# When a residual stream kept by columns is read back by rows: the read-back and the first output columns' evacuation moved in a hand-kept order

## The chip, the cores and the metric

The kernel runs on one core of one Trainium2 chip. The metric is the device time of one execution, in microseconds; the runs of the kernel before took 957.2 (median of 3; 956.22 to 961.8). Traces are of one profiled execution; their times count from the start of its span.

## The reference

Two layers of a decoder trunk on x of 256 tokens x 1024 features, all in f32:

```python
for l in range(DEPTH):                     # DEPTH = 2
    x = x + 0.5 * swiglu(rmsnorm(x, ffn1_norm[l]), ffn1_w_gate[l], ffn1_w_up[l], ffn1_w_down[l])
    ...                                    # a token mixer, then attention on a memory of 256 rows
    x = x + 0.5 * swiglu(rmsnorm(x, ffn2_norm[l]), ffn2_w_gate[l], ffn2_w_up[l], ffn2_w_down[l])
return rmsnorm(x, final_norm)

def swiglu(x, w_gate, w_up, w_down):
    return (jax.nn.silu(x @ w_gate) * (x @ w_up)) @ w_down
```

The hidden width of each SwiGLU is 2816, that is 22 tiles of 128. The change lies in the very last of these stages, ffn2 of layer 1, with the final rmsnorm behind it.

## The kernel before, in words

**Precision and weights.** Each f32 product is made of three fast ones: both sides are split into a high part and a rest. The weights stream through one ring: SP's queue loads chunks of 1 MB into tiles named raw (4 buffers, `_load_to`, L113 to L118, three chunks ahead), and for each block of 8 weight tiles ACT writes the high part whi (L143) and DVE the rest wlo (L144), five blocks deep. A block can be split when PE has let go of the block five before it. PE then runs three matmuls for each product (L575 to L577 in the gate and up products, L684 to L686 in some of them, L791 to L793 in the down product of the last stage).

**The residual x** is kept with features on the partitions and tokens along them. The last stage is different: its down product (`down_tok`, L769) puts tokens on the partitions, so that the rows of the result can be written out directly. For that x itself is needed by tokens. This is done in three steps: `to_tokens` (L508) turns two feature tiles at a time on DVE in 32x32 pieces and stores them on SP's queue into a DRAM tile, tok (L514, four times); `from_tokens` (L836) reads tok back with four DMAs on POOL's queue (L839) into a tile of the name bias; `natural(k)` (L844) copies each of the eight feature tiles k, for both halves of the tokens u, on ACT (L847) into the tile y, which has the name k2 and appears as k in the trace.

**The hidden tiles h** take a similar way. When a group of four (the last: two) hidden tiles is there by tokens, `turned_back` (L540) turns it on DVE (L545), stores it to a DRAM tile, turn (L547), reads it back with four DMAs (L549, all on POOL's queue), and some time later splits it on ACT and DVE into h (L557, L558). The six groups use the tile names v, kT, v, k2, kT, v in turn.

**The down product** has two column halves. First columns 0 to 511, for u = 0 and 1, two hidden tiles at a time: eleven parts; part i needs h of hidden tiles 2i and 2i + 1, so the eleventh part needs the group that is turned last. Then columns 512 to 1023: one long part for the first 14 hidden tiles (three regions: u = 0 whole, u = 1 in two halves of 256), and the last eight hidden tiles region by region. `evac_tok` (L800) evacuates a finished region: it adds half of the product to y (L804), sums y's squares (L807), multiplies by the final gain (L810 on POOL for the first columns), and, with the last region of a row, raises the mean to the power -1/2 on POOL (L813), scales (L817 on ACT, L820 on DVE) and writes out (L818, L821).

**What sets the order.** `Order` (L200) writes the program out with a clock of its own. Fillers are the parts of the products, each with a cost in ns (L582, L690, L798); a task given to `pe.after(delay, fn, cost)` runs, between two fillers, once the clock has passed its due time; of several due tasks the one with the earlier due time comes first. A part of the down product is not started before its h tiles have been split (`have`, L741). In the last stage the clock starts at 0 with the first gate product. Each of the 43 fillers of the gate and up products costs 2600; the norm's sums cost 250; a part of the first down columns costs 2616; the long part of the other columns 14 x 1308.

The order in which the instructions are written is not fully the order in which they run: when the program is built, a scheduler orders each engine's instructions by its own estimates of when their inputs are there, and takes the one written first when several are. An instruction wrapped in `tc.keep_in_program_order` is held behind the instruction that was written just before it on its engine. The read-back DMAs (L839) and the splits of h (L557, L558) are held so; the copies (L847), the evacuation and, in this stage, the weight splits are not.

Due times around the change, in ns of the order's clock: `from_tokens` 93000 after the stage's start; `natural(k)` 27000 + 1500 k after `from_tokens` ran; the split of the last two groups of h 22000 after they were turned; the evacuation of a region at once, with the part that finishes it.

Of the kernel before, what the change touches and what calls it, by code (L numbers as in the profile page):

```python
# [240 lines left out]
def paired(t):  # L241

    return t.rearrange("p (b a) -> p a b", b=2)
# [22 lines left out]
def build(nc, tc, ctx, a):  # L266
# [18 lines left out]
    def w2():  # L285
        return act.tile([P, 512], F32, name="w2", bufs=6)
# [28 lines left out]
    pe = Order()  # L315
# [192 lines left out]
    def to_tokens(tok, k):  # L508


        t = act.tile([P, 2 * S], F32, name="q2", bufs=2)
        tc.keep_in_program_order(nc.vector.transpose(t.rearrange("q (a g j) -> q g a j", a=4, g=4),
                                                     x[:, k:k + 2].rearrange("p k (u a i) -> p (k u) a i", u=2, a=4)))
        tc.keep_in_program_order(nc.sync.dma_start(tok[k // 2], t))  # L514
# [19 lines left out]
    def ffn(which, layer, n, nxt, first=False, last=False):  # L534
# [206 lines left out]
        def have(ks):  # L741
            return lambda: math.inf if any(h[k] is None for k in ks) else 0.0
# [26 lines left out]
        def down_tok():  # L769

            late = 2 * (ws.BUFS - 1)
            pss, got, mean = {}, {}, [EPS, EPS]

            def part(fs, *regions):

                c = regions[0][1] // 512

                def go():  # L780
                    for f in fs:
                        if (f, c) not in got:
                            got[f, c] = ws.take(f"{which}_w_down", layer, f * P, c * 512, 4)
                        for reg in regions:
                            u, c0, c1 = reg
                            if f == 0:
                                pss[reg] = (sc_tile if c == 1 and c1 - c0 == 512 else acc_tile)()[:, :c1 - c0]
                            ps = pss[reg]
                            wh, wl = (paired(w)[:, (c0 - c * 512) // 2:(c1 - c * 512) // 2] for w in got[f, c])
                            hh, hl = (h[f].v[:, u, m] for m in range(2))  # L790
                            nc.tensor.matmul(ps, hh, wh, start=f == 0, stop=False)  # L791
                            nc.tensor.matmul(ps, hh, wl, start=False, stop=False)
                            nc.tensor.matmul(ps, hl, wh, start=False, stop=f == FT - 1)  # L793
                    if fs[-1] == FT - 1:
                        for u, c0, c1 in regions:
                            evac_tok(u, slice(c0, c1), pss[u, c0, c1])

                return have(fs), go, sum(len(fs) * (c1 - c0) * 654 // 512 for _, c0, c1 in regions)  # L798

            def evac_tok(u, at, ps):  # L800
                xtok = back["y"]
                y = xtok[:, u, at]
                g = gfin[at.start // 512][:, at.start % 512:at.start % 512 + at.stop - at.start]
                nc.vector.scalar_tensor_tensor(y, ps, 0.5, y, op0=ALU.mult, op1=ALU.add)  # L804
                ms = act.tile([P, 1], F32, name="mean", bufs=4)
                junk = w2()[:, :at.stop - at.start]
                nc.vector.tensor_tensor_reduce(junk, y, y, 1.0 / D, mean[u], ALU.mult, ALU.add, ms)  # L807
                mean[u] = ms
                if at.stop < D:
                    nc.gpsimd.tensor_tensor(y, y, g, op=ALU.mult)  # L810
                    return
                r = act.tile([P, 1], F32, name="rcol", bufs=2)
                nc.gpsimd.tensor_tensor(r, ms, mhalf[:, 0:1], op=ALU.pow)  # L813
                nc.vector.tensor_tensor(y, y, g, op=ALU.mult)
                out = a["out"][u * P:(u + 1) * P]
                cuts = (0, 384, 704, D)
                nc.scalar.activation(xtok[:, u, :cuts[1]], xtok[:, u, :cuts[1]], AF.Copy, scale=r)  # L817
                nc.scalar.dma_start(out[:, :cuts[1]], xtok[:, u, :cuts[1]])  # L818
                for i, j in zip(cuts[1:], cuts[2:]):
                    nc.vector.tensor_scalar(xtok[:, u, i:j], xtok[:, u, i:j], r, None, op0=ALU.mult)  # L820
                    nc.sync.dma_start(out[:, i:j], xtok[:, u, i:j])  # L821

            end = range(FT - late, FT)
            right = ((0, 512, D), (1, 512, 768), (1, 768, D))
            return [part(range(i, i + 2), (0, 0, 512), (1, 0, 512)) for i in range(0, FT, 2)] + [
                part(range(FT - late), *right)] + [part(end, reg) for reg in right]
# [5 lines left out]
        if last:  # L832
            gfin = []
            tok, back = dram.tile([KT // 2, P, 2 * S], F32, name="tok"), {}

            def from_tokens():  # L836
                t = act.tile([P, 2 * D], F32, name="bias", bufs=1)
                for b in range(4):
                    tc.keep_in_program_order(nc.gpsimd.dma_start(  # L839
                        t[32 * b:32 * b + 32].rearrange("i (g z) -> i g z", g=16),  # L840
                        tok.rearrange("k (p i) (a z) -> a i (k p) z", p=4, a=4)[b]))
                v = t.rearrange("q (k p m u j) -> q u k m p j", k=4, p=4, m=2, u=2)

                def natural(k):  # L844
                    y = back["y"] = back.get("y") or act.tile([P, 2, D], F32, name="k2", bufs=1)
                    for u in range(2):
                        nc.scalar.activation(y[:, u, k * P:(k + 1) * P].rearrange("q (p j) -> q p j", p=4),  # L847
                                             v[:, u, k // 2, k % 2], AF.Copy)

                for k in range(KT):  # L850
                    pe.after(27000 + 1500 * k, lambda k=k: natural(k), 0)

            def last_factors():
                gfin.extend(act.tile([P, 512], F32, name="p2", bufs=4) for _ in range(2))
                src = a["final_norm"]
                for i, g in enumerate(gfin):
                    nc.sync.dma_start(g, bass.AP(tensor=src.tensor, offset=src.offset + i * 512, ap=[[0, P], [1, 512]]))

            pe.after(90000, last_factors, 0)
            for k in range(0, KT, 2):  # L860
                pe.after(16000 + 9000 * (k // 2), lambda k=k: to_tokens(tok, k), 0)
            pe.after(93000, from_tokens, 0)
        at = AT.get((which, layer))
        groups = [f0 for f0 in range(0, FT, 4) if at is None or f0 != SEVEN]
        ups = [f for f0 in groups for f in hidden(f0)]
# [504 lines left out]
    pe.after(60000, mem_scale, 0)  # L1370
    pe.after(100000, lambda: early.update(bias=load_bias(0)), 0)
    ffn("ffn1", 0, n, nxt, first=True)
    bias, sinks = early["bias"], (vecs[:, VCOL["sinks"]:VCOL["sinks"] + 8], nsinks)

# [11 lines left out]
    memory(0, n, nxt, keys[0])  # L1386
    n, nxt = nxt, xn(("ffn1_norm", 1))
    ffn("ffn2", 0, n, nxt)
    n, nxt = nxt, xn(("mix_norm", 1))
    pe.after(114000, lambda: early.update(bias=load_bias(1)), 0)  # L1390
    ffn("ffn1", 1, n, nxt)
    n, nxt = nxt, xn(("xa_norm", 1))
    odd_mixer(n, nxt, early["bias"], mem_keys(1))
# [73 lines left out]
```

## Time and profile before

| what | value |
| --- | --- |
| median of the runs | 957.2 us (956.22, 957.2, 961.8) |
| the profiled execution's own time | 956.5 us |
| its span | 954.5 us |
| granted TensorE clock, mean over the span | 0.998 |
| PE busy | 945.7 us, 99% |
| DVE busy | 726.4 us, 76% |
| ACT busy | 596.8 us, 63% |
| POOL busy | 118.0 us, 12% |
| DMA, mean | 247 GB/s |

How to read the rows that follow. In an order of time a row has the start in us, the duration in us, the engine, the line, the operation, output<-input with the program's tile names, the shapes, xN for N instructions run together, and in brackets the idle time of the engine just before it and what ended that. In a table by stretch each row has the stretch, its length, then for PE, PEld (the weight loads), DVE, ACT and POOL the busy us and the number of instructions, then the granted TensorE clock, the DMA share and GB/s. In the chain of waits a row has start, duration and what the end of the program was waiting for at that time. "DMA to landing" is the time from the issue of a DMA to the landing of its last byte.

### The profile page before, as it was taken

The numbers are of one execution on the slowest core, as the hardware profiler recorded it, in microseconds if no ns is written. First come the engines' busy times: TensorE is split into PE (matmuls) and PEld (weight loads), VectorE is DVE, ScalarE is ACT, GpSimd is POOL, SyncE is SP. The second block draws the span as 40 slices with busy tenths as digits, with TensorE's granted clock in tenths as the row PEclk, the third lists the DMA queues.
The fourth block names the chain that finished last, engine by engine and source line by source line (L and its number), as shares of the span: only waits on it lengthen the run. The fifth ranks groups of instructions, "written<-read, shape, count | busy, mean of one in ns | idle before, by whom it ended". The sixth has DMA issues, their size and how long they took to land.

```text
span 954.5 us, 15174 instructions
## 1 busy us (share of the span) xinstructions
PE 945.7 (99%) x5796; PEld 866.9 (91%) x5796; DVE 726.4 (76%) x1153; ACT 596.8 (63%) x984; POOL 118.0 (12%) x207
## 2 busy tenths in 40 slices
PE   9999999999999999999999999999999999999997
PEld 8888899999999888889988888999999998888896
DVE  7667667798878886976778697687877789769583
ACT  7555555697657865655577565456785688565551
POOL 0412210001000110221001111200000001202311
PEclk9999999999999999999999999999999999999999
DMA  9999875455536889989768978855644388999851
GB/s 369 330 357 322 311 234 218 170 187 195 184 134 243 231 259 301 302 290 349 245 196 242 333 246 270 323 200 181 239 147 167 113 288 259 292 322 329 255 189 45
DMA packets 39368, 235.44 MB, mean 247 GB/s; under 512 B 5624, under 2 KB 6648, under 8 KB 14720
## 3 DMA queue, kind: packets, MB, share of 16 engines
q1 hardware_dynamic: 26928, 182.43, 52.1%
q0 software_dynamic: 11792, 51.42, 20.5%
q8 instruction: 45, 0.74, 0.3%
q10 hardware_dynamic: 576, 0.64, 0.2%
q14 instruction: 27, 0.22, 0.1%
HBM read 220.81 MB, written 16.80 MB: 249 GB/s over the span
## 4 chain that ended last, share of the span: by engine, by line
PE 95%; DMA 2%; ACT 1%; DVE 0%; POOL 0%; issue 0%; POOLq 0%; SPq 0%; DVEq 0%; ACTq 0%
PE acc L576 11%; PE acc L577 11%; PE acc L575 11%; PE acc L418 8%; PE acc L423 7%; PE acc L425 7%; PE acc L424 7%; PE acc L419 4%; PE sc L418 3%; PE tr L685 2%; PE tr L684 2%; PE tr L686 2%; PE sc L575 2%; PE sc L576 2%; PE sc L577 2%; PE sc L419 2%
## 5 line engine op out<-in xcount | busy, mean ns | idle before, releaser
L144 DVE TENSOR_TENSOR wlo<-raw,whi 128x1024 fp32r<-128x1024 f32 (+2 forms) x363 | 409.4, 1140 | 153.9 <-ACT whi L143 151.4
L143 ACT ACTIVATE whi<-raw 128x1024 fp32r<-128x1024 f32 (+2 forms) x363 | 353.4, 986 | 238.4 <-PE acc L577 81.8
L576 PE MATMUL acc<-wlo,x 128*128 128x512 f32 x528 | 200.5, 380 | 0.2
L577 PE MATMUL acc<-whi,x 128*128 128x512 f32 x528 | 199.9, 379 | 0.0
L575 PE MATMUL acc<-whi,x 128*128 128x512 f32 x528 | 195.3, 380 | 0.0
L576 PEld LDWEIGHTS acc<-wlo,x 128*128 128x128 f32 x528 | 99.8, 189 | 15.7 <-DVE wlo L144 1.7
L575 PEld LDWEIGHTS acc<-whi,x 128*128 128x128 f32 x528 | 99.7, 189 | 14.1 <-ACT whi L143 0.2
L577 PEld LDWEIGHTS acc<-whi,x 128*128 128x128 f32 x528 | 99.8, 189 | 14.0
L418 PE MATMUL acc<-h,whi 128*128 128x512 f32 x330 | 108.6, 382 | 0.0
L419 PE MATMUL acc<-h,wlo 128*128 128x256 f32 x330 | 89.9, 273 | 0.0
L425 PE MATMUL acc<-h,wlo 128*128 128x256 f32 x322 | 87.7, 275 | 0.0
L424 PE MATMUL acc<-h,whi 128*128 128x256 f32 x322 | 87.7, 275 | 0.0
L423 PE MATMUL acc<-h,whi 128*128 128x256 f32 x322 | 86.5, 277 | 0.0
L425 PE MATMUL acc<-x,wlo 128*128 128x256 f32 x304 | 84.1, 278 | 0.0
L424 PE MATMUL acc<-x,whi 128*128 128x256 f32 x304 | 83.8, 277 | 0.0
L423 PE MATMUL acc<-x,whi 128*128 128x256 f32 x304 | 83.3, 278 | 0.0
L418 PEld LDWEIGHTS acc<-h,whi 128*128 128x128 f32 x330 | 62.4, 189 | 8.6
L419 PEld LDWEIGHTS acc<-h,wlo 128*128 128x128 f32 x330 | 63.3, 192 | 0.2
L424 PEld LDWEIGHTS acc<-h,whi 128*128 128x128 f32 x322 | 61.7, 192 | 0.1
L425 PEld LDWEIGHTS acc<-h,wlo 128*128 128x128 f32 x322 | 61.7, 192 | 0.1
L423 PEld LDWEIGHTS acc<-h,whi 128*128 128x128 f32 x322 | 60.6, 192 | 0.4 <-DVE x L486 0.2
L424 PEld LDWEIGHTS acc<-x,whi 128*128 128x128 f32 x304 | 58.2, 192 | 0.2
(274 smaller groups left out, 1730.8 us busy)
## 6 DMA issues: line engine op xcount, KB each, us to landing
raw<-in_w SPq DMA_DIRECT2D x165, 1024.0 KB, 6.8
bias<-in_w POOLq DMA_DIRECT2D x12, 1024.0 KB, 12.6
k<-in_w POOLq DMA_DIRECT2D x9, 1024.0 KB, 9.1
turn<-v POOLq DMA_DIRECT2D x9, 512.0 KB, 3.3
v<-turn POOLq DMA_DIRECT2D x36, 128.0 KB, 6.5
dists<-line POOLq DMA_DIRECT2D x2, 1536.0 KB, 14.1
raw<-in_memT SPq DMA_DIRECT2D x3, 1024.0 KB, 4.7
turn<-kT POOLq DMA_DIRECT2D x6, 512.0 KB, 10.6
```

Source lines behind the costliest of these rows:

```text
L143: for ins in (self.nc.scalar.activation(hi[:, at], src, AF.Copy), self.nc.vector.tensor_tensor(lo[:, at], src, hi[:, at].bitcast(F32), op= ...
L144: self.nc.vector.tensor_tensor(lo[:, at], src, hi[:, at].bitcast(F32), op=ALU.subtract)):
L418: nc.tensor.matmul(ps, w[0], x2.both, start=start, stop=False)
L419: nc.tensor.matmul(ps[:, :S], w[1], x2.high, start=False, stop=stop)
L423: nc.tensor.matmul(ps[:, :S], w[0], x2.high, start=start, stop=False)
L424: nc.tensor.matmul(ps[:, :S], w[0], x2.low, start=False, stop=False)
L425: nc.tensor.matmul(ps[:, :S], w[1], x2.high, start=False, stop=stop)
L575: nc.tensor.matmul(ps[u], xh, wh, start=k == 0, stop=False)
L576: nc.tensor.matmul(ps[u], xh, wl, start=False, stop=False)
L577: nc.tensor.matmul(ps[u], xl, wh, start=False, stop=k == KT - 1)
L684: nc.tensor.matmul(ps, xh, wh, start=p == 0, stop=False)
L685: nc.tensor.matmul(ps, xh, wl, start=False, stop=False)
```

## The change

Three delays in `ffn` change, all of them in the last stage. The read-back of x by tokens is due at 114500 in place of 93000, which is after the clock at which the last group of hidden tiles is turned. The copies are due 15000 + 700 k after the read-back in place of 27000 + 1500 k. The evacuation of a region is now a task of its own: due 6000 after the end of its part for the first columns (c = 0), and at once, but still as a task, for the others. No instruction is added or taken away.

```diff
@@ down_tok, part
                     if fs[-1] == FT - 1:
                         for u, c0, c1 in regions:
-                            evac_tok(u, slice(c0, c1), pss[u, c0, c1])
+                            pe.after(0 if c else 6000, lambda u=u, at=slice(c0, c1), ps=pss[u, c0, c1]: evac_tok(u, at, ps), 0)
@@ from_tokens
                 for k in range(KT):
-                    pe.after(27000 + 1500 * k, lambda k=k: natural(k), 0)
+                    pe.after(15000+700*k, lambda k=k: natural(k), 0)
@@ ffn, last
             for k in range(0, KT, 2):
                 pe.after(16000 + 9000 * (k // 2), lambda k=k: to_tokens(tok, k), 0)
-            pe.after(93000, from_tokens, 0)
+            pe.after(114500, from_tokens, 0)
```

## The prediction

> **What bounds the kernel now.** I read the page first, then a table by stretch of the last down stage, then PE's order in time around the one hole that it shows, the chain of waits through it, and the orders on ACT, POOL and DVE.
>
> ```profile
> span 954.5 us, 15174 instructions
> PE 945.7 (99%) x5796; PEld 866.9 (91%) x5796; DVE 726.4 (76%) x1153; ACT 596.8 (63%) x984; POOL 118.0 (12%) x207
> ```
>
> The span holds 8.8 us in which PE is not busy (954.5 - 945.7). Whatever the change does on other engines counts only where it opens or closes a hole in PE. Where are the holes in the stretch that the change touches? The table by stretch gives PE's busy time first, the DMA share and GB/s last.
>
> ```profile
> 880.00:890.00 10.00, 10.00 (x48) 8.76 (x47) 6.05 (x10) 4.10 (x9) 5.34 (x9) 1.00 1.04 277
> 890.00:900.00 10.00, 10.00 (x48) 8.75 (x47) 5.11 (x10) 6.04 (x21) 0.94 (x2) 1.00 0.82 270
> 900.00:905.00 5.00, 4.31 (x21) 3.45 (x19) 3.20 (x5) 3.65 (x10) 2.22 (x5) 1.00 0.79 216
> 905.00:920.00 15.00, 15.00 (x74) 13.23 (x73) 12.64 (x17) 9.63 (x12) 1.76 (x4) 1.00 0.92 347
> 920.00:947.00 27.00, 27.00 (x187) 25.37 (x186) 14.63 (x18) 6.98 (x7) 5.50 (x4) 1.00 0.04 16
> ```
>
> One hole only, between 900 and 905. PE's order in time shows it, with what the wait was for:
>
> ```profile
> 901.45 0.38 PE L793 MATMUL acc<-whi,h 128*128 128x512 f32 x1
> 901.67 0.38 PE L791 MATMUL acc<-whi,h 128*128 128x512 f32 x1
> 902.74 0.48 PE L792 MATMUL acc<-wlo,h 128*128 128x512 f32 x1 [0.69 <-DVE wlo L144]
> 903.06 0.38 PE L793 MATMUL acc<-whi,h 128*128 128x512 f32 x1
> ```
>
> From 901.67 to 903.06 are 1.39 us for two steps that take 0.216 each elsewhere (901.45 to 901.67, for one), so this hole costs 1.39 - 0.43 = **0.96 us**. The chain of waits leads from it back to the change's subject:
>
> ```profile
> 882.49 1.93 POOL bias L839 x3
> 884.42 12.64 DMA bias<-tok
> ...
> 900.48 0.96 ACT whi L143
> ...
> 901.46 1.24 DVE wlo L144
> ```
>
> The read-back of x by tokens (L839) lands at 897.1, its sixteen copies (L847) stand on ACT ahead of the next weight split (L143), and PE eats up the splits made in advance. ACT's order of time says how long that was:
>
> ```profile
> 878.56 1.06 ACT L143 ACTIVATE whi<-raw 128x1024 fp32r<-128x1024 f32 x1 [1.53 <-PE acc L577]
> 881.15 1.06 ACT L143 ACTIVATE whi<-raw 128x1024 fp32r<-128x1024 f32 x1 [1.53 <-PE acc L577]
> ...
> 892.15 1.06 ACT L143 ACTIVATE whi<-raw 128x1024 fp32r<-128x1024 f32 x1
> 897.16 3.31 ACT L847 ACTIVATE k<-bias 128x128 f32<-128x128 f32 x16 [3.96 <-DMA bias<-tok]
> 900.38 1.99 ACT L143 ACTIVATE whi<-raw 128x1024 fp32r<-128x1024 f32 x2
> 903.72 1.34 ACT L557 ACTIVATE h<-kT 128x256 fp32r<-128x256 f32 x4 [1.34 <-DMA kT<-turn]
> ...
> 909.00 0.73 ACT L557 ACTIVATE h<-v 128x256 fp32r<-128x256 f32 x2 [1.10 <-DMA v<-turn]
> ```
>
> One block of weights lasts 2.59 us (878.56 to 881.15). ACT waited 3.96 us for the landing and copied for 3.31; a copy is 3.31 / 16 = 0.207 us. So the most that the change can win here is 0.96 us, 0.1% of the time.
>
> **The change part by part.** *The read-back moves behind the last turned tile.* The order clock runs with the matmuls: the stage's first matmul and the first of the down columns are
>
> ```profile
> 776.90 0.38 PE L575 MATMUL acc<-whi,x 128*128 128x512 f32 x1
> ...
> 888.72 0.38 PE L791 MATMUL acc<-whi,h 128*128 128x512 f32 x1
> ```
>
> 111.82 us apart, and the 43 fillers between them cost 43 x 2600 = 111800, so one tick is one ns; with the 250 of the norm's sums the last tile is turned at clock 112050. Due 93000 ran after filler 36 (93850); due 114500 runs after the first down part (112050 + 2616 = 114666). On POOL the four DMAs now come after the two last turned tiles:
>
> ```profile
> 872.62 0.56 POOL L547 DMA_DIRECT2D turn<-k  x1 [3.43 <-DVE k L545]
> 880.30 2.19 POOL L549 DMA_DIRECT2D k<-turn  x4 [7.12 <-ACT whi L143]
> 882.48 2.59 POOL L839 DMA_DIRECT2D bias<-tok  x4
> 887.47 0.57 POOL L547 DMA_DIRECT2D turn<-kT  x1 [2.40 <-DMA k<-turn]
> 899.06 2.19 POOL L549 DMA_DIRECT2D kT<-turn  x4 [11.01 <-ACT k L847]
> 901.23 0.56 POOL L547 DMA_DIRECT2D turn<-v  x1
> 904.58 2.18 POOL L549 DMA_DIRECT2D v<-turn  x4 [2.78 <-ACT h L557]
> ...
> 881.25 0.70 DVE L545 STREAM_TRANSPOSE kT<-w 128x512 f32<-128x512 f32 x1
> ...
> 894.07 0.45 DVE L545 STREAM_TRANSPOSE v<-w 128x256 f32<-128x256 f32 x1
> ```
>
> The new order, worked forward. Tile kT is turned by 881.95 and POOL is free at 882.49, so turn<-kT goes at 882.5. It lands, by the k tile's row (872.62 to 880.30), 7.7 later: 890.2. Its four reads are issued by 892.4. Tile v is turned at 894.52; turn<-v goes then and lands, by its own row (901.23 to 904.58), 3.35 later: 897.9. Its reads are issued by 900.1. Then the read-back: first DMA at 900.1, the last started 1.95 later (three quarters of its 2.59) at 902.05. The view of that tile's instructions says how long the four take:
>
> ```profile
> DMA to landing us min/median/max: 8.1/10.9/12.6
> ```
>
> From the last one's start that bounds the landing to 910.1 (8.1) and 914.7 (12.6). I take 9.5, nearer the low end: the 8.1 to 12.6 were paid at a DMA share of 1.04 (880 to 890, above), while the stretch after 900 has 0.79, and what lies ahead in POOL's queue is now the half-width v tile. **Landing at 911.5**, 14 us later than before. If turn<-kT again waits as at 887.47, kT's reads end at 887.5 + 7.7 + 2.2 = 897.4, all is about 3 us later, and the latest landing is 917.6.
>
> The Trainium skill's DMA: Bandwidth & Descriptors (Anatomy of one DMA) fits a transfer on GpSimd's path by about 2.0 us plus the bytes at 436 GB/s. For these 256 KB that is an estimate of 2.6 us, the landing would be 904.7 and nothing would wait; the trace differs, with at least 8.1 for the same transfer, and I go by the trace.
>
> *Who waits for the landing.* The copies are due 15000 + 700k after 114666, the split of the last tile (L557) at 112050 + 22000 = 134050; copy pair k = 6 is due at 133866, so the pinned split is written, and so issued, behind fourteen copies. PE needs that split for the eleventh pair of rows, at 888.72 + 10 x 2.59 = 914.6 (without a hole). Fourteen copies are 2.90 us and the first half of the split is 0.73 / 2 = 0.37, so the landing must come by 914.6 - 3.3 = **911.3**; each weight split that ACT runs among them (1.06) takes its time off that: 910.3 with one. My 911.5 gives a wait of 0.2 to 1.2; I take 0.7. Also queued behind the first copy on ACT are the weight splits from about the eleventh block on (five buffers, one block per 2.59 us), and DVE's wlo behind them; they need the same 914.6, so they add nothing of their own.
>
> *The hole at 902* goes whole: nothing then stands on ACT between 893.2 and 900 but weight splits. -0.96.
>
> *DMAs freed and loaded.* From 882 to 897 the raw loads on SP's queue have the read-back out of their way; PE had no other hole there, so 0. Around 900 to 912 they share with it; a raw load late by as much as the read-back's own 12.6 would still lie inside three chunks of lead (two blocks each, 15.5 us), so 0, and one chunk's lateness if that lead is gone.
>
> *The first down columns' evacuation* is due 6000 after clock 140826, and the next part costs 14 x 1308 = 18312, so it is written at 159138, behind every weight split that is left.
>
> ```profile
> 918.00 1.28 DVE L804 SCALAR_TENSOR_TENSOR k<-acc,k 128x512 f32<-128x512 f32 x2
> ...
> 935.26 1.23 DVE L144 TENSOR_TENSOR wlo<-raw,whi 128x1024 fp32r<-128x1024 f32 x1 [1.41 <-ACT whi L143]
> 941.99 0.69 DVE L804 SCALAR_TENSOR_TENSOR k<-sc,k 128x512 f32<-128x512 f32 x1 [5.50 <-PE sc L793]
> ...
> 920.03 3.83 POOL L810 TENSOR_TENSOR k<-k,p 128x512 f32<-128x512 f32 x2 [13.27 <-ACT whi L143]
> 943.62 1.02 POOL L813 TENSOR_TENSOR rcol<-mean,mhalf 128x1 f32<-128x1 f32 x1 [19.76 <-DVE mean L807]
> ```
>
> At the earliest it stays at 918. At the latest it follows the last wlo: 936.5, plus 1.28, about as much again for its two sums of squares, and POOL's 3.83, ending near 943, before POOL's 943.62. Between 920 and 947 PE has no hole to close, so 0 either way. The price without that cover is one for one on the tail. Its real use is as a guard: with copies that end at 911.5 + 3.3 + about 2 = 917, they are just ahead of it.
>
> **Sum:** -0.96 + 0.7 = -0.3 us. The profiled execution took 956.5 (span 954.5 and 2.0 around it), so 956.2 for it; the median of the runs is 0.7 above, 957.2, which gives **956.9**.
>
> **The rivals.** *All of it is won:* the landing comes by 910.3, no new wait, -0.96: 956.2. For it speaks that the weight loads at 900 to 905 leave the DMAs at 0.79; against it that 8.1 was the best of four. *The new wait outgrows the old one,* slower: place ACT, copies in front of the last tile's split; it decides from a landing after 911.3 + 0.96 = 912.3 (911.2 with a weight split between). At 915 (about the 12.6 of before) the wait is 3.7 to 4.7, net +2.7 to +3.7, some 960.4; at 917.6 it is +5.3 to +6.3, up to 963.5. For it speaks that copying the old duration gives 914.7; against it that the load is lighter.
>
> The Trainium skill's TensorE: Matmul & The Clock Gate (Part 1) has PE's clock halved after an idle window of about 3.4 us and back after as long. By that rule a wait of 3.7 or more would cost an estimated 1.7 us on top, 962 instead of 960.4. The trace's 0.96 us hole left the granted clock at 1.00; no longer hole stands in this stage to test it.
>
> *The copies are placed too early on ACT:* the build may move them forward (in the trace they ran ahead of splits written before them). Ahead of the tenth block's split, due at 912.0, that block's wlo would end at 911.5 + 3.31 + 0.96 + 1.24 = 917.0; wait 4.8 (its second matmul wants it), net +3.8: 961.0. Against it: DMAs that are issued at 900 can hardly be thought landed two blocks before. *It doesn't do what it says:* another wait on ACT (for kT's landing, 1.34 us ahead of 903.72) keeps the hole at 902: 957.2.
>
> **How the numbers follow.** Forecast 0.42 (its own range 956.2 to 957.8), all won 0.23, outgrown 0.22, too early 0.08, no effect 0.05. The range runs from all won less 0.6 for the runs' scatter, 955.6, to the slow side at a landing near 916, 961.5; left out are its last part and scatter, some 0.15. About 1%, 9.6 us, can be told from no change: a gain cannot reach it (0.96), so faster 0.01; slower needs a landing past 921, 0.02; within 1% 0.97.
>
> **What would show it.** Right: no hole at 902; L839 after v's last L549, issued 899 to 903; L847 waiting on the read-back until 910 to 913; PE's next hole, if any, at 914 to 916, on h or wlo, under 1.5 us; L804 and PE's end moved by less than 1 us. Wrong: a hole of over 2 us near 915 (late landing), one between 905 and 912 (copies placed too early), or L839 before 895 (the tiles turn faster than I think).

## The result, and the profile after

The changed kernel takes 964.6 us (median; 958.5 to 968.9) beside 957.2 for the kernel before: 1.0073 times as long, with an interval of 1.0056 to 1.009. (One execution of 1093 us, in which the mean granted clock was 0.85, is left out.) That is 0.7% slower, and 3.1 us above the upper end of the forecast range.

The profiled execution took 960.96 us, 4.5 more than before's 956.5. Its page and its table by stretch, with the same columns as in the prediction:

```profile
span 958.9 us, 15176 instructions
PE 947.4 (99%) x5796; PEld 868.9 (91%) x5796; DVE 726.1 (76%) x1153; ACT 596.6 (62%) x984; POOL 119.2 (12%) x207
```

```profile
890.00:900.00 10.00, 10.00 (x48) 8.77 (x47) 5.70 (x9) 3.60 (x6) 2.74 (x5) 1.00 0.74 233
900.00:905.00 5.00, 5.00 (x25) 4.38 (x24) 3.88 (x7) 4.76 (x8) 3.95 (x7) 1.00 0.68 244
905.00:920.00 15.00, 11.50 (x50) 9.67 (x49) 4.19 (x6) 6.31 (x22) 0.81 (x2) 0.94 0.68 205
920.00:947.00 27.00, 27.00 (x167) 24.72 (x167) 17.92 (x18) 10.13 (x10) 3.83 (x2) 0.97 0.21 78
```

The hole of 900 to 905 is gone (5.00 busy of 5.00), and a larger one stands in 905 to 920 (11.50 of 15.00). The column after POOL, the granted clock, falls below 1.00 in the same stretch. Of the 4.4 us of longer span 2.7 are PE's idle time (11.5 in place of 8.8). PE's busy time takes the other 1.7 (947.4 against 945.7, for the same 5796 matmuls): matmuls that ran longer, not more of them. PE's order of time around the hole shows both:

```profile
914.38 0.38 PE L793 MATMUL acc<-whi,h 128*128 128x512 f32 x1
918.26 0.79 PE L791 MATMUL acc<-whi,h 128*128 128x512 f32 x1 [3.50 <-ACT h L557]
918.85 0.63 PE L792 MATMUL acc<-wlo,h 128*128 128x512 f32 x1
...
921.71 0.38 PE L793 MATMUL acc<-whi,h 128*128 128x512 f32 x1
```

From 914.38 to 918.26 are 3.88 us for a step of 0.216: a hole of 3.66. The next eight steps, 918.26 to 921.71, take 3.45 in place of 8 x 0.216 = 1.73: another 1.72. The granted clock of these steps, third from the end of the row, is about half:

```profile
918.00:920.00 2.00, 1.74 (x4) 1.46 (x5) 0.87 (x3) 2.00 (x6) 0.00 (x0) 0.54 0.00 0
```

With the old hole of 0.96 gone, 3.66 + 1.72 - 0.96 = 4.42, which is the whole of the longer span. The wait is for h, the split of the last turned tile, as the bracket says. The chain of waits and ACT's order of time lead back from it:

```profile
905.16 9.73 DMA bias<-tok
```

```profile
901.48 4.83 ACT L143 ACTIVATE whi<-raw 128x1024 fp32r<-128x1024 f32 x5
915.00 2.90 ACT L847 ACTIVATE k<-bias 128x128 f32<-128x128 f32 x14 [8.69 <-DMA bias<-tok]
917.81 0.70 ACT L557 ACTIVATE h<-v 128x256 fp32r<-128x256 f32 x2
```

ACT sat idle for 8.69 us in front of fourteen copies, whose input landed at 914.9. Behind them stood the split (L557), and PE went on at 918.26, 3.26 after the first copy. Why the landing was so late is in POOL's order of time:

```profile
883.67 0.56 POOL L547 DMA_DIRECT2D turn<-kT  x1
892.63 2.19 POOL L549 DMA_DIRECT2D kT<-turn  x4 [8.40 <-ACT w L607]
894.81 0.56 POOL L547 DMA_DIRECT2D turn<-v  x1
901.05 2.18 POOL L549 DMA_DIRECT2D v<-turn  x4 [5.68 <-ACT h L557]
903.23 2.59 POOL L839 DMA_DIRECT2D bias<-tok  x4
926.47 3.83 POOL L810 TENSOR_TENSOR k<-k,p 128x512 f32<-128x512 f32 x2 [20.65 <-ACT whi L143]
```

An L547 row is the store of a turned tile, the L549 row behind it begins when that store has landed, so the difference of the two starts is the time of the store. (In both L549 rows the bracket names ACT; it was long done, and the store was what POOL waited for.) The two stores took 8.96 (883.67 to 892.63) and 6.24 us (894.81 to 901.05), and the read-back was issued at 903.23.

### The profile page after: what moved, and what is told of

It is laid out like the page before. It is cut to its first block, busy times and chain, and to the rows that moved or that the text cites. A ratio compares the mean times of both kernels' runs of the same rounds, so it can differ in the third digit from the quotient of the medians.

```text
span 958.9 us, 15176 instructions
## 1 busy us (share of the span) xinstructions
PE 947.4 (99%) x5796; PEld 868.9 (91%) x5796; DVE 726.1 (76%) x1153; ACT 596.6 (62%) x984; POOL 119.2 (12%) x207
## 6 DMA issues: line engine op xcount, KB each, us to landing
bias<-in_w POOLq DMA_DIRECT2D x12, 1024.0 KB, 12.5
```

## The experiments

**The theory** after this result: the whole loss is ACT's queue. The copies' input lands too late, ACT runs its instructions in their order, and whatever PE needs next stands behind the copies; the idle PE then also loses half its clock for a few us. **The rivals:** that the later copies or the later evacuation cost something by themselves; that only the last split counts and not the weight splits behind the copies; that the read-back disturbs the other DMAs wherever it stands, so that no better place for it is to be had; and that the clock is most of it.

| kernel | what differs from the changed kernel | median, us | ratio to before (95%) |
| --- | --- | --- | --- |
| e1 | read-back at its old time | 956.8 | 0.9977 to 1.0012 |
| e3 | last split due ahead of the copies | 963.1 | 1.002 to 1.0084 |
| e4 | e1, copies held in written order | 959.5 | 1.0018 to 1.0043 |
| e6 | read-back issued from ACT's queue | 959.5 | 1.0014 to 1.004 |
| e10 | read-back between the last two turned tiles | 962.6 | 1.0026 to 1.0069 |
| e11 | copies held behind the last split | 959.0 | 1.0003 to 1.0045 |
| e12 | copies held behind seven more weight splits | 956.0 | 0.9981 to 1.0016 |
| e7, r3 | copies on POOL (twice) | 956.2, 955.7 | 0.9975 to 1.0009, 0.9979 to 0.9999 |
| e5, r2 | PE kept busy in the hole (twice) | 962.2, 961.1 | 1.0043 to 1.0082, 1.0033 to 1.0074 |
| r1 | nothing | 965.7 | 1.0077 to 1.0117 |

### e1: the read-back at its old time, the rest of the change kept

```diff
-                    pe.after(15000+700*k, lambda k=k: natural(k), 0)
+                    pe.after(35800+700*k, lambda k=k: natural(k), 0)
@@
-            pe.after(114500, from_tokens, 0)
+            pe.after(93000, from_tokens, 0)
```

> The changed kernel with the read-back alone put back: due 93000 again, the copies still due at the same clock as in the changed kernel (129650 on), the evacuation of the first columns still 6000 later. Theory A (the copies wait on ACT for a late landing, in front of the last tile's split): the landing is back near 897, no hole of PE at 914, 957.2 (before's time), with at most before's own hole of 0.96 us near 902. Rival B (the later evacuation or the copies' later due time cost the 7 us): it stays at 963 to 965.

Measured: 956.8 us, ratio 0.9995 (0.9977 to 1.0012), no change from before. From 860 us on, the traces of e1 and of the kernel before have the same order of instructions on ACT, DVE and POOL, though the copies and the evacuation are written later in e1: the scheduler puts them back. So without the late read-back the two other edits do nothing, and there is no loss. What they do beside a late read-back e1 doesn't test; for the place of the copies e11 and e12 below do.

### r1 and e5, r2: the changed kernel again, and with PE kept busy in the hole

e5 and r2 are the changed kernel with 16 products of zeros ahead of the eleventh part, on a tile that nothing reads. (One more line of the edit, not shown, writes the loop over the regions more shortly and does the same. The trace lists 32 matmuls for the 16 products.)

```diff
-                    for f in fs:
+                    for f, pt in zip(fs, [(c == 0 and fs[-1] == FT - 1) and tr_tile()] + [None] * 30):
+                        for _ in range(16 if pt else 0): tc.keep_in_program_order(nc.tensor.matmul(pt[:, :P], zeros, zeros, start=True, stop=True))
```

> The changed kernel with sixteen matmuls of zeros, which nothing reads, on PE in front of the eleventh part (about 3.6 us of work at full clock, by the 18 of 0.22 at the start of the kernel at half clock). They fill most of the hole and don't shorten the wait. If the hole's length is all (rival C): the time stays at 964.6 or is longer by what of the 3.6 us the hole doesn't cover. If PE's granted clock falls after a hole of over 3.4 us (theory A with the clock): the granted clock stays at 1.00 behind the hole, and the 1.7 us that the profile shows behind it (eight steps at 0.43 in place of 0.216) are won, 961.5 to 963.5.

> The changed kernel itself, unchanged, on the chip of the runs beside it, with a second profile. Its first profile was of one of its shortest executions (960.96 of a median of 964.6): copies released at 915.0, PE back at 918.26, eight slow steps. Theory A: in this profile PE is back 3.3 us after the landing again, whatever the landing is, and span less before's span equals the hole plus the slow steps less 0.96; 963 to 966. If the extra of the median were elsewhere (rival: a lower clock over the whole span, or earlier stages), the profile shows more than 1 us that is not in the hole and behind it.

> The changed kernel with sixteen matmuls of zeros in front of the eleventh part once more, now beside the changed kernel itself on one chip. If the clock's fall behind the hole costs 1.7 us or more: 1.7 to 3.4 us less than the changed kernel beside it. If only the hole's length counts: the same or longer.

Measured: e5 962.2, and side by side on one chip r1 965.7 and r2 961.1 (1.0097 beside 1.0053; the intervals do not overlap, though barely). That is 4.6 us less in r2, where 1.7 to 3.4 were expected; r1 has only six executions, and one execution of each has a trace, so where the landing fell in the others isn't known. The order of time in e5, on PE and on ACT:

```profile
914.69 3.73 PE L782 MATMUL tr<-const-float32-0.0 128*128 128x128 f32 x32
919.15 0.48 PE L791 MATMUL acc<-whi,h 128*128 128x512 f32 x1 [0.72 <-ACT h L557]
919.47 0.38 PE L792 MATMUL acc<-wlo,h 128*128 128x512 f32 x1
919.68 0.41 PE L793 MATMUL acc<-whi,h 128*128 128x512 f32 x1
```

```profile
915.88 2.90 ACT L847 ACTIVATE k<-bias 128x128 f32<-128x128 f32 x14 [10.29 <-DMA bias<-tok]
```

Here the landing was 0.9 us later than in the changed kernel's profile (first copy 915.88 against 915.00), and yet the execution ended 0.85 earlier (960.11 against 960.96): after the wait the matmuls ran at 0.2 to 0.3 a step at once, not at 0.43. The profile of r1 shows the opposite end:

```profile
919.68 0.80 PE L791 MATMUL acc<-whi,h 128*128 128x512 f32 x1 [4.83 <-ACT h L557]
```

```profile
916.42 2.90 ACT L847 ACTIVATE k<-bias 128x128 f32<-128x128 f32 x14 [9.49 <-DMA bias<-tok]
```

Its hole is 4.99 us, ten slow steps lose another 2.24, and 4.99 + 2.24 - 0.96 = 6.27, against a span that is 6.3 longer than before's. r2's profile fell on a late landing: zeros until 918.28, 4.57 idle, and half the clock after that, for 5.6 us (922.85 to 928.45).

```profile
914.55 3.73 PE L782 MATMUL tr<-const-float32-0.0 128*128 128x128 f32 x32
922.85 0.80 PE L791 MATMUL acc<-whi,h 128*128 128x512 f32 x1 [4.57 <-ACT h L557]
```

In all four profiles PE goes on 3.26 to 3.27 us after the first copy: the mechanism is fixed, the landing is not. First copies at 915.00, 916.42, 915.88 and 919.59 are four draws of one order of instructions.

How much of the loss is the clock? Each run lists its mean granted clock. It is 0.9953 over the runs of the changed kernel and 0.9942 in r1, but 0.9976 in e5, 0.9981 in r2 and 0.9982 in before. Taken as lost time over 960 us, an estimate, that is 2.8 us of clock between before and the changed kernel, 2.2 between the latter and e5 (their medians differ by 2.4), 3.7 between r1 and r2 (4.6). The estimate is rather high, since a clock that is low while PE is idle counts in it and costs nothing (0.82 in r1 from 914 to 919, most of it idle): for r1's profile it gives 2.9 (0.995 against 0.998), and its slow steps lost 2.24. So of the some 7 us at most about 2.8 are the clock, and the rest, with the 0.96 won added, is a wait of 5.2 or a little more: a first copy near 916.5, about the middle of the four.

### e7 and r3: the copies on POOL

```diff
-                        nc.scalar.activation(y[:, u, k * P:(k + 1) * P].rearrange("q (p j) -> q p j", p=4),
-                                              v[:, u, k // 2, k % 2], AF.Copy)
+                        nc.gpsimd.tensor_copy(y[:, u, k * P:(k + 1) * P].rearrange("q (p j) -> q p j", p=4),
+                                              v[:, u, k // 2, k % 2])
```

> The changed kernel with the sixteen copies on POOL in place of ACT; the read-back stays as late as in the changed kernel. Theory A: ACT waits for nothing, the last tile's split runs when its own read lands (906 to 908), no hole at 914 or 917; the copies run on POOL from the landing near 915 to 920 to 923, the first columns' evacuation waits for them on DVE until then, with weight splits in stock; 955.5 to 957. Rival B (DMA load from the later read-back): the time stays above 962.

> The copies on POOL once more, beside the run with the copies behind the stock and on the same chip: both keep the late read-back and free ACT's order in different ways. Theory A: both alike, 955.5 to 957, about 1 us under before (the hole at 902 is gone, none comes for it).

Measured: 956.2 (0.9992) and 955.7 (0.9989, 0.9979 to 0.9999). The loss is gone with the read-back left where the change put it. r3's order of time on POOL and its table by stretch:

```profile
916.84 4.88 POOL L847 COPY k<-bias 128x128 f32<-128x128 f32 x16 [9.47 <-DMA bias<-tok]
```

```profile
905.00:920.00 15.00, 15.00 (x71) 13.13 (x70) 10.91 (x12) 8.33 (x11) 5.53 (x14) 1.00 0.95 297
```

The landing is even later than in the changed kernel's profile, 916.84, and PE is busy for 15.00 of 15.00 at a clock of 1.00. So here neither the late landing nor any load of the DMAs costs PE time; the place of the copies on ACT does. These are the lowest medians of the study, though not told apart from e12's below: some 0.1% under the kernel before (r3's interval just excludes no change, e7's does not) and 0.8% under the changed one (0.9989 / 1.0073).

### e12 and e11: a late read-back, its copies held further back on ACT

Both hold the copies in written order, and differ by their due time:

```diff
-                        nc.scalar.activation(y[:, u, k * P:(k + 1) * P].rearrange("q (p j) -> q p j", p=4),
-                                              v[:, u, k // 2, k % 2], AF.Copy)
+                        tc.keep_in_program_order(nc.scalar.activation(
+                            y[:, u, k * P:(k + 1) * P].rearrange("q (p j) -> q p j", p=4), v[:, u, k // 2, k % 2], AF.Copy))
@@
-                    pe.after(15000+700*k, lambda k=k: natural(k), 0)
+                    pe.after(23000+700*k, lambda k=k: natural(k), 0)    # e11
+                    pe.after(28000+700*k, lambda k=k: natural(k), 0)    # e12
```

> The changed kernel with the copies due 23000 + 700 k after the read-back and held in program order: behind the last tile's split, but on ACT ten of them still in front of the twelfth block's weight split. If the last tile's split behind the copies is all (narrow): no hole, 955.5 to 957. If the weight splits behind them count as well (wide): that block's split is at landing (915 to 917) + 2.1 + 1.06, its rest 1.2 later, wanted at 917.2: a hole of 2 to 4 us near 917, with 0 to 2 us of slow clock behind it: 958 to 963.

> The changed kernel with the copies due 28000 + 700 k and held in program order, so that seven more weight splits stand in front of them on ACT; the read-back as late as in the changed kernel, copies on ACT as there. They start near 923.5, after any landing seen so far (911 to 920). Theory A: no hole at 914 or 917, the late read-back costs nothing, 955.5 to 957. If the late read-back itself costs (its load on the DMAs, the late evacuation of the first columns): over 959.

Measured: e11 959.0 (1.0024, 1.0003 to 1.0045), e12 956.0 (0.9999). ACT's and PE's order of time in e11:

```profile
905.34 0.72 ACT L557 ACTIVATE h<-v 128x256 fp32r<-128x256 f32 x2 [0.56 <-DVE wlo L144]
...
915.33 2.11 ACT L847 ACTIVATE k<-bias 128x128 f32<-128x128 f32 x10 [7.38 <-DMA bias<-tok]
917.35 4.83 ACT L143 ACTIVATE whi<-raw 128x1024 fp32r<-128x1024 f32 x5
```

```profile
918.44 0.48 PE L791 MATMUL sc<-whi,h 128*128 128x512 f32 x1 [1.11 <-ACT whi L143]
919.70 0.48 PE L792 MATMUL sc<-wlo,h 128*128 128x512 f32 x1 [0.78 <-DVE wlo L144]
```

The last split ran ten us ahead of the copies, and PE still stopped, one block later, for the weight splits that stood behind them. So freeing the split alone isn't enough. In e12 the copies ran behind seven more weight splits than in e11, without any wait, and PE had no hole in 905 to 920 either. ACT's order of time, and the table by stretch:

```profile
924.01 3.29 ACT L847 ACTIVATE k<-bias 128x128 f32<-128x128 f32 x16
```

```profile
905.00:920.00 15.00, 15.00 (x77) 13.26 (x76) 7.83 (x7) 6.18 (x6) 0.00 (x0) 1.00 0.95 306
```

The two runs have the read-back as late as the changed kernel, and lose 2 us and nothing where that loses 7. So the loss of 7 takes both: a late landing, and copies that stand ahead of the last split and of the weight splits behind it. The change's read-back with before's own delays of the copies, 27000 + 1500 k, was not run.

### e3: the last split due ahead of the copies

```diff
-            pe.after((34000 if f0 < 8 else 28000 if f0 < SEVEN else 22000) if sevens else
+            pe.after((34000 if f0 < 8 else 28000 if f0 < SEVEN else 17000 if last and f0 + 4 > FT else 22000) if sevens else
```

> The changed kernel with the last tile's split due 17000 after it was turned in place of 22000, so that it is written ahead of the copies and not behind fourteen of them. If the order behind the copies is all that holds PE (theory A, narrow), the hole at 914 goes and the time is 956 to 957. If the copies hold the weight splits as well (theory A, wide): the eleventh block's rows are there, but the weight split of the twelfth block is behind sixteen copies on ACT; it comes at landing + 3.3 + 1.06, its rest 1.2 later, PE wants it at 917.2, so with a landing of 915 a hole of about 3.3 us at 917 in place of 3.7 at 914, and 960 to 964. Rival B (DMA load): no change, 964.6.

Measured: 963.1 (1.0052), hardly better, and the hole stood in another place than expected. ACT's and PE's order of time:

```profile
914.06 0.72 ACT L557 ACTIVATE h<-v 128x256 fp32r<-128x256 f32 x2 [11.59 <-DMA v<-turn]
914.69 2.93 ACT L143 ACTIVATE whi<-raw 128x1024 fp32r<-128x1024 f32 x3
```

```profile
915.78 0.80 PE L791 MATMUL acc<-whi,h 128*128 128x512 f32 x1 [6.52 <-ACT whi L143]
```

Now the split itself waited for its own input: the reads of v, issued at 902.73 just ahead of the read-back at 904.90, landed only at 914.0, and three weight splits stood behind it. Putting another late reader first moves the hole; it doesn't close it. Why these reads took 11.3 us is open: in e11, with the read-back just as close behind them, they were issued at 901.37 and their split ran at 905.34. With five executions, one of them at 956.2, e3's time isn't told apart from the changed kernel's.

### e4, e6, e10: other places for the read-back

e4 is e1 with the copies held in written order, so that weight splits stand between them. e6 changes the queue, e10 the due time:

```diff
-                    tc.keep_in_program_order(nc.gpsimd.dma_start(
+                    tc.keep_in_program_order(nc.scalar.dma_start(          # e6
@@
-                    pe.after(15000+700*k, lambda k=k: natural(k), 0)
+                    pe.after(27000+700*k, lambda k=k: natural(k), 0)       # e10
@@
-            pe.after(114500, from_tokens, 0)
+            pe.after(102500, from_tokens, 0)                               # e10
```

> The read-back as early as before (due 93000), the copies held in program order on ACT, due 129650 on, spread between weight splits, the evacuation later. The landing stays near 897 and nothing stands on ACT for it. Theory A: no hole near 902 nor at 914; 0.96 us under before: 955.5 to 956.5. Rival B (POOL's order: the read-back in front of kT's and v's tiles makes those late, and now ACT waits for them): a hole of the order of 1 us stays, 956.5 to 957.5.

> The changed kernel with the four read-back DMAs issued from ACT's own queue in place of POOL's, at the same written place (clock 114666, near 892), so that they don't wait behind kT's and v's reads on POOL; copies on ACT as in the changed kernel. If the late landing comes from the place in POOL's queue (theory A), they land some 9 to 12 us after 892, by 901 to 904, the copies end by 908, no hole at 914: 955.5 to 957. If it comes from the load on the DMAs in that stretch, landing at 908 or later and a hole: over 958.

> The read-back due 102500, behind kT's and in front of v's tile on POOL, the copies due 27000 + 700 k after it (the same clock as in the changed kernel), copies on ACT. By theory A the landing is issue (895) plus 10 to 13, 905 to 908, about 8 us before the changed kernel's, and PE needs the first of what stands behind it no sooner than 909 to 912: 956.5 to 959. By the rival that the transfer hinders whoever is near it (the run on ACT's queue: turn<-v took 12 us): v's tile comes late, about 914 to 917, and a hole of 1 to 3 us stays at the eleventh part: 958 to 961.

Measured: 959.5 (1.0031), 959.5 (1.0027) and 962.6 (1.0048); none is as good as the kernel before, and e4 and e10 lie above everything that I expected of them (at most 957.5 and 961). In e4 ACT stood at the split of v until its reads had landed, with five weight splits behind it:

```profile
913.26 0.72 ACT L557 ACTIVATE h<-v 128x256 fp32r<-128x256 f32 x2 [3.69 <-DMA v<-turn]
914.29 4.83 ACT L143 ACTIVATE whi<-raw 128x1024 fp32r<-128x1024 f32 x5
```

That profile is of a short execution (957.3): PE waited 1.4 us in it, in two holes, against 0.7 in before. What the longer executions of e4 lose more isn't shown.

In e6 the read-back was issued at 889 to 891 and in e10 at 895.73, both ahead of the last tile's store. POOL's order of time in e6, and in e10:

```profile
892.64 0.56 POOL L547 DMA_DIRECT2D turn<-v  x1 [0.29 <-DVE v L545]
904.77 2.17 POOL L549 DMA_DIRECT2D v<-turn  x4 [11.57 <-ACT whi L143]
```

```profile
895.73 2.59 POOL L839 DMA_DIRECT2D bias<-tok  x4
898.30 0.57 POOL L547 DMA_DIRECT2D turn<-v  x1
910.43 2.18 POOL L549 DMA_DIRECT2D v<-turn  x4 [11.55 <-DMA turn<-v]
```

That store took 12.1 us in both, against 6.24 in the changed kernel with nothing of the read-back beside it. It isn't what stopped PE, though: in both the split of v ran without a wait, at 911.46 and 916.10. In e10 the copies again stood waiting for their own landing (909.0), and a weight split behind ten of them left PE a hole of 4.06 us:

```profile
909.10 2.10 ACT L847 ACTIVATE k<-bias 128x128 f32<-128x128 f32 x10 [4.91 <-issue]
911.11 1.04 ACT L143 ACTIVATE whi<-raw 128x1024 fp32r<-128x1024 f32 x1
916.10 0.71 ACT L557 ACTIVATE h<-v 128x256 fp32r<-128x256 f32 x2
```

```profile
912.20 0.80 PE L791 MATMUL acc<-whi,h 128*128 128x512 f32 x1 [4.06 <-ACT whi L143]
```

In e6 ACT waited for the reads of kT, and then for the copies' landing, with a weight split behind each; PE's three holes there have waits of 0.59 to 0.78 us:

```profile
902.09 1.34 ACT L557 ACTIVATE h<-kT 128x256 fp32r<-128x256 f32 x4 [8.78 <-DMA kT<-turn]
905.41 2.51 ACT L847 ACTIVATE k<-bias 128x128 f32<-128x128 f32 x12 [1.04 <-DMA bias<-tok]
907.82 1.04 ACT L143 ACTIVATE whi<-raw 128x1024 fp32r<-128x1024 f32 x1
```

Of the rival of the disturbed neighbour one half holds for these places: issued ahead of the last tile's store, the read-back goes with a late store. The other half, that PE then waits for that store, doesn't. What PE waited for was again weight splits behind something on ACT that waited for a DMA, in e10 the copies themselves.

## Why the prediction was wrong

**What failed** is the landing at 911.5, above all the step "turn<-v goes then and lands, by its own row, 3.35 later". Step by step, forecast and profile: turn<-kT issued 882.5, was 883.67; its landing 7.7 later, was 8.96; turn<-v issued 894.5, was 894.81, since the 2 us of slack that POOL had there took up the lateness so far; its landing 3.35 later, was **6.24**; read-back issued 900.1, was 903.23; last of the four started 902.05, was 905.16; landing 9.5 later, was 9.73. Of the 3.4 us by which the landing missed (914.9 for 911.5) 2.9 are the store of v. The 3.35 was one draw. In the nine profiles whose read-back stands behind it, the changed kernel's among them, this store took between 4.8 and 7.1 us (e3 902.73 - 897.97, r3 902.61 - 895.53). The 9.5 was too short as well: from the start of the last read-back DMA to the landing the four profiles of the changed kernel's order (it, r1, e5, r2) have 9.7, 10.4, 11.6 and 12.5, and 6.2, 6.6, 6.9 and 5.8 for the store. Their middles put the landing of a median execution some 3.1 + 1.5 us later than forecast, an estimate, that is near 916, where the profiled one had 914.9. The forecast's landing was thus about the best of what came: as the first copy shows it, 911.3 in e7, 915.0 to 919.6 in the others that waited for it. That the load would be light was right (0.74 and 0.68 in the table by stretch) and proved nothing: the store of v took 6.24 us there, and 3.35 in before at a share of 0.79.

**What was left out of the sum** is the clock. It stood beside the rival "the new wait outgrows the old one" as the Trainium skill's rule and not in the forecast, because before's trace has no hole long enough. The rule (the Trainium skill's TensorE: Matmul & The Clock Gate, Part 1: half the clock after an idle window of about 3.4 us, full again after as long) agrees with the changed kernel's trace: a hole of 3.66 us, then eight steps at about 0.43 for 3.45 us. The estimate of 1.7 us on top was 1.72. In r2 the clock came back later than that, 5.6 us after the end of a wait of 4.57. The range left the clock out as well: its slow side, 961.5 at a landing near 916, would by the 2.8 above have been some 964.

**What was right:** the hole at 902 went whole (5.00 of 5.00), worth 0.96. The release is the landing plus 3.3: 3.26 to 3.27 in four profiles, and PE's need at 914.6 (914.38 + 0.22). With the landing that came, the same working gives a wait of 914.9 - 911.3 = 3.6, measured 3.66; the rival "the new wait outgrows the old one" is what came, and its net of +2.7 for a landing at 915, with its 1.7 of clock, gives 960.9 on before's profiled 956.5, where 961.0 was measured. The later evacuation cost nothing: e12 has it too (L810 at 927.57) and no loss. With the late landing the evacuation did move by 6.4 us (L810 at 926.47, before 920.03), not by less than 1, with nothing on PE behind it. The build did not move the copies ahead of the tenth block's split, so that rival fell.

**What was too narrow:** weight splits behind the copies "add nothing of their own", since "they need the same 914.6". In the trace the eleventh block had been split ahead of the copies; those behind begin with the twelfth, needed one block later, at 917.2. Where the last split waits there too, they add nothing; in e11, without it, they stopped PE by themselves. The slow side was given 0.22; what spoke for it was that the range of the landing, 910.1 to 917.6, lay for five sixths beyond the 911.3 at which the wait begins. I took a value near the early end of each DMA instead of the middle of the rows.

What stays open is why the store of v takes 3.35 us in one profile and 7.1 in another, and so why one program's landing spreads over some 5 us. With the clock behind it, that is the likely cause of the spread of its runs, 958.5 to 968.9, but only two of them have a trace.

## What to carry to other kernels

An instruction that waits for a DMA holds up everything behind it on its engine: put it behind as much finished stock as the DMA can be late (e12), or on an engine that nothing urgent uses (e7), rather than guess the landing. Where a chain has several DMAs in a row, take each from the middle or the late end of the rows, since the late end is what PE sees, and never all from the early end. And count the clock behind a long hole in PE: here holes of 3.66 and 4.99 us cost about half as much again (1.72 and 2.24 us).

## What the runs showed of the hardware

**The clock fell after two short pauses.** In e11 PE paused for 1.27 us (916.95 + 0.22 to 918.44) and, one step later, 1.04 (918.66 to 919.70); with 0.22 of work between them neither is near the 3.66 of the changed kernel. The table by stretch of e11 around them, with the clock third from the end:

```profile
918.00:920.00 2.00, 0.78 (x2) 0.48 (x3) 1.58 (x2) 2.00 (x3) 0.00 (x0) 1.00 0.00 0
920.00:922.00 2.00, 2.00 (x10) 1.86 (x9) 2.00 (x3) 2.00 (x3) 0.00 (x0) 0.58 0.62 160
922.00:924.00 2.00, 2.00 (x10) 1.82 (x9) 2.00 (x3) 0.17 (x1) 0.00 (x0) 0.57 1.00 414
```

In e6 two pauses that lie as close, but with waits of 0.59 and 0.78 us in place of 1.11 and 0.78, left it at 1.00. So a single pause as long as the changed kernel's 3.66 wasn't needed here; that the little work within a few us decided is an inference, and no run was made for it.

**A store takes longer with the read-back just ahead of it.** The store of v took 12.1 us with the read-back in flight (e6, e10), whichever queue issued that, and 3.35 to 7.1 in the twelve profiles where it had landed or was still to come. The store of kT, twice the size, took 11.0 to 11.6 us just behind the read-back (before, e1, e4) and 6.9 to 9.7 in the eleven others. Which resource the two share no run here shows.
